# A two-layer attention trunk: the value products of a head pair issued later, its eviction put first on VectorE

## The chip, the cores and the metric

The kernel runs on one core of one Trainium2 chip. The metric is device time in microseconds (us) of one execution; the time before is the median of three runs. The core's engines are TensorE (PE in the profile, with its weight loads as a row of their own, PEld), VectorE (DVE), ScalarE (ACT), GpSimd (POOL) and SyncE (SP), which issues the DMAs.

## The reference, cut to what matters

Two layers run over 512 positions of width 1024. Each layer has a sparse-attention branch (eight heads of 64, in two groups) and a gated linear-attention branch; the change touches the first. Its output per head is a gated sum of three attentions: over compressed keys, over selected blocks, over a window.

```
out = gt[..., 0:1] * o_c + gt[..., 1:2] * o_s + gt[..., 2:3] * o_w
o_nsa = o_nsa * silu(p_nz)
y = m_nsa * (o_nsa @ w_up_nsa) + m_gla * (o_gla @ w_up_gla)
x = x + rms(y @ w_out, g_post)
```

At this length every block is selected and the window covers all earlier positions, so both `o_s` and `o_w` are causal attentions over all 512 positions, with different keys and values.

## The kernel before, in words

All matrices are 32-bit; a product is made with three matmuls, from a high part and a low part (what rounding left over) of each operand: high by high, high by low, low by high (`split3`, lines 175 to 179). A high part is a ScalarE copy, a low part a subtraction on VectorE or GpSimd.

**Attention.** The eight heads are taken in four pairs p (heads p and p + 4). A pair has five steps: `cmp_steps` (compressed keys) and four `attn_steps`, for the two halves ip of the query blocks (i = 0, 1 and i = 2, 3) and the two branches br. `cmp_steps` has three parts: scores and softmax; transposes; and the start of the pair's accumulator `acc` with two matmuls (lines 918, 919). `attn_steps` has three parts: the scores of its first block, those of its second, and the value products (line 998). After the scores `weigh` makes the softmax on VectorE and ScalarE, `turn` transposes it on VectorE into a tile T, writes T to DRAM (line 940) and reads it back rearranged as `W`, a tile of the pool PT, with four DMAs (lines 942, 943). The value products of half 0 are 8 matmuls per branch, those of half 1 are 16; all add into `acc`, a PSUM tile of a pool with one buffer. When the last are done (half 1, branch 1), `acc` is evicted: VectorE multiplies it into `f_` (line 1003), ScalarE takes the high part H (line 1005), GpSimd the low part Lo (line 1006). Pool PT holds two buffers for each half.

**Order.** TensorE's order is the program's, written by hand. The loop at lines 1038 to 1062 goes through 20 steps, n = 5p + m, and calls the parts with `go`; between them `fill` issues matmuls of other projections as gap filler, by a credit in us from the table `FILL`, one row per m, four gaps a row. The other engines' queues (SyncE's too) are ordered by the compiler, which takes what it finds ready in order of priority; priority is program order unless something is put ahead with `tc.high_priority()`. Weight loads (line 136) have three landing buffers, `raw`; one is free when ScalarE and VectorE have split the weights in it (lines 153, 154). They are issued on SyncE, as are the DMAs of `turn`.

**After the loop** the rest of the filler is issued (`need("ug7")`), then the gate projections of the first two output units `un0` and `un1`, then the last pair's second-half values, then the rest of the units. `up` (lines 731 to 746) makes a unit: 24 matmuls of a gate, then 12 of the up-projection over the four pairs' outputs `oTn`, the last pair's (k = 3) last.

Of the kernel before, what the change touches and what calls it, by code (L numbers as in the profile page):

```python
# [9 lines left out]
F32 = mybir.dt.float32  # L10
# [4 lines left out]
OP = mybir.AluOpType  # L15
# [52 lines left out]
def trunk(ctx, tc, x, wpk, sp, gvec, cs, wa, out):  # L68
# [23 lines left out]
    def new(pl, shape=(128, 512), dt=F32, tag=None, bufs=None):  # L92
        cnt[0] += 1
        kw = {} if bufs is None else {"bufs": bufs}
        return sb[pl].tile(list(shape), dt, tag=tag or pl, name=f"{tag or pl}_{cnt[0]}", **kw)

    def ps(tag):
        cnt[0] += 1
        return psp[tag].tile([128, 512], F32, tag=tag, name=f"ps_{tag}_{cnt[0]}")
# [4 lines left out]
    mm, tp = nc.tensor.matmul, nc.tensor.transpose  # L104
    V, A, G = nc.vector, nc.scalar, nc.gpsimd
# [65 lines left out]
    def get(l, n, ahead=2):  # L171
        issue(POS[l, n] + ahead)
        return ready.pop((l, n))

    def split3(o, w, h, first, last):

        mm(o, w[0], h[0], start=first, stop=False)  # L177
        mm(o, w[0], h[1], start=False, stop=False)  # L178
        mm(o, w[1], h[0], start=False, stop=last)  # L179

    def fm(l, n, hT, then):

        w = get(l, n)
        o = ps("mm")
        for k in range(KT):
            if type(w) is list:
                wk = [t[:, k % 4 * 128:(k % 4 + 1) * 128] for t in w[k // 4]]
            else:
                wk = [t[:, k * 128:(k + 1) * 128] for t in w]
            split3(o, wk, hT(k), k == 0, k == KT - 1)  # L190
            if k == KT - 1:
                then(o)
            yield 0.64
# [118 lines left out]
    for l in range(L):  # L312
# [21 lines left out]
        def fill(us):  # L334
            credit[0] += us
            while credit[0] > 0.3 and queue:
                credit[0] -= step(*queue[0])

        def step(name, gen):
            try:  # L340
                return next(gen)
            except StopIteration:
                queue.pop(0)
                done.add(name)
                return 0.0

        def need(name):
            while name not in done:
                step(*queue[0])
# [343 lines left out]
        PR = [[None, None, None, None] for _ in range(4)]  # L693
# [37 lines left out]
        def up(f, gate, wn, src, then):  # L731
            th = []

            def sig(o):
                th.append(new("th"))
                A.activation(th[0], o, AF.Tanh, scale=0.5)

            yield from fm(l, f"{gate}{f}", hT, sig)
            w = get(l, f"{wn}{f}")
            u = ps("mm")  # L740
            for k in range(4):
                sl = slice(k * 128, (k + 1) * 128)
                split3(u, (w[0][:, sl], w[1][:, sl]), src[k], k == 0, k == 3)
                if k == 3:
                    then(th[0], u)
                yield 0.64
# [31 lines left out]
        for f in range(8):  # L778
            put(f"ug{f}", up(f, "mgg", "ug", oTg, take_ug))
# [144 lines left out]
        def turn(p, br, i, pps):  # L924

            ip, n = i // 2, i + 1
            r = (4 * ip + 3) * 64
            if i % 2 == 0:  # L930
                TT[p, br] = new("T", (128, 4, r), tag=f"T{ip}")
            T = TT[p, br]
            t = T[:, :, (i % 2) * i * 64:((i % 2) * i + n) * 64].rearrange("p b (j g q) -> p b j g q", j=n, g=2)
            for g in range(2):
                V.transpose(t[:, :, :, g], pps[g][:, :n * 128].rearrange("p (j b q) -> p b j q", j=n, b=4))  # L935
            if i % 2:
                cnt[0] += 1
                dr = dram.tile([128, 4, r], F32, tag=f"tp{ip}", name=f"tp_{cnt[0]}", bufs=2)
                with tc.issue_after(back[-1]) if back else nullcontext():
                    dma(dr, T)  # L940
                W = PT[p, br, ip] = new("PT", (128, 4, r), tag=f"PT{ip}")
                for b in range(4):
                    back.append(dma(W[b * 32:(b + 1) * 32], dr[:, b].rearrange("(a k) r -> k a r", a=4)).ins)

        def scores(p, i, brs):

            w = (i + 1) * 128
            ww = w * len(brs)  # L950
            both = len(brs) > 1
            nsc[0] += 1
            o = [ps("ts"[nsc[0] % 2]) for _ in range(2)]
            for g in range(2):
                for n in range(2):
                    kn = first[g][:, n].rearrange("p b n -> p (b n)") if both else keys[brs[0]][g][n][:, :w]
                    mm(o[g][:, :ww], PR[p][1][g][:, i * 128:(i + 1) * 128], kn, start=(n == 0), stop=(n == 1))  # L957
            pps = [weigh(p, g, i, brs, o[g]) for g in range(2)]
            turn(p, brs[0], i, [t[0] for t in pps])
            if both:  # L960
                held[p] = [t[1] for t in pps]
# [18 lines left out]
        def attn_steps(p, ip, br):  # L980
            for i in (2 * ip, 2 * ip + 1):
                if i or not br:
                    scores(p, i, (br,) if i else (0, 1))
                else:
                    turn(p, br, i, held.pop(p))
                yield

            acc, W = PR[p][3], PT[p, br, ip]
            i0 = 2 * ip
            for j in range(i0 + 2):  # L990
                for g in range(2):
                    c0 = br * 128 + g * 64
                    if j <= i0:
                        m = W[:, :, :2 * (i0 + 1) * 64].rearrange("p a (i j g q) -> p i a j g q", i=2, g=2, q=32)
                        m, w = m[:, :, :, j, g], 256
                    else:
                        m, w = W[:, :, (2 * j) * 64 + g * 32:(2 * j) * 64 + g * 32 + 32], 128
                    mm(acc[g * 64:(g + 1) * 64, (i0 + 2) * 128 - w:(i0 + 2) * 128],  # L998
                       vsw[j // 2][:, j % 2, c0:c0 + 64], m,
                       start=False, stop=(br == 1 and j == i0 + 1), skip_group_check=True)  # L1000
            if ip == 1 and br == 1:
                f_ = new("p")
                V.scalar_tensor_tensor(f_, acc, 0.5, PR[p][2], op0=OP.mult, op1=OP.mult)
                H, Lo = new("oT", dt=F32R), new("oT", dt=F32R)
                A.copy(H, f_)  # L1005
                G.tensor_tensor(Lo, f_, H.bitcast(F32), op=OP.subtract)  # L1006
                oTn[p] = (H, Lo)
            yield

        steps = []  # L1010
        for p in range(4):
            steps.append((p, cmp_steps, ()))
            steps += [(p, attn_steps, (ip, br)) for ip in range(2) for br in range(2)]
        live = [f(p, *a) for p, f, a in steps]

        def go(n):
            if 0 <= n < len(steps):
                next(live[n])
# [19 lines left out]
        for n in range(len(steps)):  # L1038
            m = n % 5
            f4 = FILL[m]  # L1040
            if m == 0:
                need(f"q{steps[n][0]}")
            if m == 4:
                need(f"nz{steps[n][0]}")
            go(n)
            if m == 3:
                go(n - 5)
                go(n - 4)
            fill(f4[0])
            if m == 2:  # L1050
                go(n - 2)
            fill(f4[1])
            if m != 0:
                go(n)
                fill(f4[2])
            if m == 3:
                go(n - 3)
            if m == 4:
                go(n - 3)
                go(n - 2)  # L1060
            fill(f4[3])
        need("ug7")

        uns = [up(f, "mgn", "un", oTn, take_un(f)) for f in range(8)]
        for f in range(2):
            for k in range(KT):
# [8 lines left out]
        src = x if l == 0 else x1  # L1075
# [6 lines left out]
        for s in range(ST):  # L1082
# [22 lines left out]
            for h, c0, c1 in pieces:  # L1105
                V.scalar_tensor_tensor(xh[h][:, c0:c1], tt[h][:, c0:c1], rs[:, 0:1], xh[h][:, c0:c1],  # L1106
                                       op0=OP.mult, op1=OP.add)
# [80 lines left out]
```

## Time and profile before

| | |
|---|---|
| runs before | 809.73, 810.62, 812.09 us; median 810.62 |
| profiled execution, its own time | 808.68 us |
| its span, first to last instruction | 807.0 us |
| mean granted TensorE clock | 0.997 |
| TensorE busy | 789.5 us (98%) |
| VectorE busy | 553.5 us (69%) |
| ScalarE, GpSimd busy | 354.4 us (44%), 97.6 us (12%) |

Times of single instructions are from the profiled execution, in us from the start of its span. A matmul's busy time overlaps that of the next one, so a run of matmuls is read by the distance of their starts. The two layers show the same pattern; attention is about 142 to 310 in the first and 537 to 704 in the second.

### The profile page before, as it was taken

What the parts mean: (1) busy time and instruction counts of PE and PEld (TensorE: products, weight loads), DVE (VectorE), ACT (ScalarE), POOL (GpSimd) and SP (SyncE); (2) the same over time, 40 slices, a digit from 0 to 9 for tenths busy, and PEclk for the clock granted to TensorE, in tenths of its full rate; (3) what the DMA queues carried; (4) which work ended last, traced back from release to release, by engine and by line L of the source; (5) the groups of instructions that cost most, each with busy time, mean ns of one, the idle gap of its engine ahead of it and who ended that gap; (6) DMA issues with size and microseconds to landing.
All of it is one profiled execution on the core that took longest, in us unless ns stands there. A gap on an engine that the chain in (4) does not pass through costs nothing. (4 is left out here: it accounts for less than half of the span.)

```text
span 807.0 us, 12043 instructions
## 1 busy us (share of the span) xinstructions
PE 789.5 (98%) x4262; PEld 644.4 (80%) x4262; DVE 553.5 (69%) x1274; ACT 354.4 (44%) x731; POOL 97.6 (12%) x117
## 2 busy tenths in 40 slices
PE   8999999999989999999999999999999999999996
PEld 5888788887878887888898878888877788788885
DVE  6753749999998945645574366589999987366223
ACT  5671236554554524442356413556555444245211
POOL 3000024000010102211010102311000101032100
PEclk9999999999999999999999999999999999999998
DMA  6641124367676773446246121234767677545222
GB/s 233 229 147 58 53 67 130 105 191 217 183 236 204 235 227 119 153 153 223 79 129 212 52 78 54 83 114 149 223 201 215 214 212 222 171 157 158 78 105 79
DMA packets 54272, 124.04 MB, mean 154 GB/s; under 512 B 6562, under 2 KB 23490, under 8 KB 54212
## 3 DMA queue, kind: packets, MB, share of 16 engines
q1 hardware_dynamic: 54064, 123.01, 48.4%
q8 instruction: 34, 0.56, 0.3%
q10 hardware_dynamic: 148, 0.27, 0.1%
q14 instruction: 26, 0.21, 0.1%
HBM read 94.94 MB, written 25.17 MB: 149 GB/s over the span
## 5 line engine op out<-in xcount | busy, mean ns | idle before, releaser
L177 PE MATMUL ps_mm<-hT,hl 128*128 128x512 f32 x544 | 217.5, 400 | 0.0
L178 PE MATMUL ps_mm<-hT,hl 128*128 128x512 f32 x544 | 212.5, 391 | 0.0
L179 PE MATMUL ps_mm<-hT,hl 128*128 128x512 f32 x544 | 212.3, 390 | 0.0
L153 ACT CAST hl<-raw 128x1024 fp32r<-128x1024 f32 (+3 forms) x107 | 97.6, 915 | 138.3 <-PE ps_mm L178 99.9
L154 DVE TENSOR_TENSOR hl<-raw,hl 128x1024 fp32r<-128x1024 f32 (+3 forms) x107 | 117.4, 1098 | 47.6 <-ACT hl L153 42.5
L177 PEld LDWEIGHTS ps_mm<-hT,hl 128*128 128x128 f32 x544 | 102.2, 188 | 23.3 <-issue 3.1
L179 PEld LDWEIGHTS ps_mm<-hT,hl 128*128 128x128 f32 x544 | 102.2, 188 | 22.1
L178 PEld LDWEIGHTS ps_mm<-hT,hl 128*128 128x128 f32 x544 | 102.4, 188 | 19.0
L972 ACT ACTIVATE g<-g,sx 128x128 f32<-128x128 f32 (+3 forms) x128 | 71.0, 555 | 67.9 <-DVE sx L970 67.5
L935 DVE STREAM_TRANSPOSE T<-g 128x256 f32<-128x256 f32 (+3 forms) x128 | 58.6, 491 | 0.7
L975 DVE TENSOR_SCALAR g<-g,sx,gt 128x128 f32<-128x128 f32 (+3 forms) x128 | 57.0, 459 | 1.5
L178 PE MATMUL ps_mm<-oT,hl 128*128 128x512 f32 x128 | 50.3, 393 | 1.7 <-POOL oT L1006 1.7
L177 PE MATMUL ps_mm<-oT,hl 128*128 128x512 f32 x128 | 50.9, 398 | 0.0
L179 PE MATMUL ps_mm<-oT,hl 128*128 128x512 f32 x128 | 49.9, 390 | 0.0
L1006 POOL TENSOR_TENSOR oT<-p,oT 128x512 fp32r<-128x512 f32 x8 | 14.3, 1784 | 239.0 <-ACT oT L1005 239.0
L998 PE MATMUL ps_o<-PT,a 128*64 128x256 f32 (+1 forms) x384 | 38.6, 348 | 3.9 <-DMA PT<-tp 3.9
L998 PEld LDWEIGHTS ps_o<-PT,a 128*64 128x64 f32 x384 | 25.4, 137 | 18.3 <-issue 9.4
L200 POOL TENSOR_TENSOR rs<-ms,mhalf 128x1 f32<-128x1 f32 (+1 forms) x24 | 17.2, 719 | 177.0 <-DVE ms L198 175.3
L1026 POOL TENSOR_TENSOR p<-p,g 128x512 f32<-128x512 f32 x16 | 28.0, 1750 | 84.3 <-DVE p L1025 72.7
L970 DVE CUSTOM_DVE_ANT_0 g<-ps_t,cmask 128x256 f32<-128x256 f32 (+3 forms) x64 | 28.8, 477 | 2.3 <-PE ps_t L957 2.2
L970 DVE CUSTOM_DVE_ANT_0 g<-ps_s,cmask 128x128 f32<-128x128 f32 (+3 forms) x64 | 29.0, 481 | 1.7 <-PE ps_s L957 1.7
L178 PEld LDWEIGHTS ps_mm<-oT,hl 128*128 128x128 f32 x128 | 24.1, 188 | 6.5 <-POOL oT L1006 2.3
(269 smaller groups left out, 1313.3 us busy)
## 6 DMA issues: line engine op xcount, KB each, us to landing
raw<-wpk SPq DMA_DIRECT2D x96, 512.0 KB, 3.8
tp<-T SPq DMA_DIRECT2D x16, 896.0 KB, 4.1
PT<-tp SPq DMA_DIRECT2D x64, 224.0 KB, 4.9
raw<-wpk SPq DMA_DIRECT2D x32, 256.0 KB, 3.0
tp<-T SPq DMA_DIRECT2D x16, 384.0 KB, 2.5
PT<-tp SPq DMA_DIRECT2D x64, 96.0 KB, 2.4
a<-wpk SPq DMA_DIRECT2D x16, 256.0 KB, 5.7
p<-x SPq DMA_DIRECT2D x16, 256.0 KB, 2.9
```

Of the source, the lines that this page charges most:

```text
L153: A.copy(H[:, :w], r[:, :w])
L154: V.tensor_tensor(Lo[:, :w], r[:, :w], H[:, :w].bitcast(F32), op=OP.subtract)
L177: mm(o, w[0], h[0], start=first, stop=False)
L178: mm(o, w[0], h[1], start=False, stop=False)
L179: mm(o, w[1], h[0], start=False, stop=last)
L200: G.tensor_tensor(r[:, :n], ms[:, :n], mhalf[:, :n], op=OP.pow)
L935: V.transpose(t[:, :, :, g], pps[g][:, :n * 128].rearrange("p (j b q) -> p b j q", j=n, b=4))
L970: V.tensor_tensor_reduce(pp[:, :w], ob, cmask[:, 512 - w:512], 1.0, -3 * NEG, OP.add, OP.min, sx[:, 0:1])
L972: A.activation(pp[:, :w], pp[:, :w], AF.Exp, bias=sx[:, 0:1], scale=-1.0, accum_out=sx[:, 1:2])
L975: V.tensor_scalar(pp[:, :w], pp[:, :w], sx[:, 2:3], gt[:, i, h * 3 + 1 + br:h * 3 + 2 + br], op0=OP.mult, op1=OP.mult)
L998: mm(acc[g * 64:(g + 1) * 64, (i0 + 2) * 128 - w:(i0 + 2) * 128], vsw[j // 2][:, j % 2, c0:c0 + 64], m, start=False, stop=(br == 1 and j = ...
L1026: G.tensor_tensor(t_, t_, y2[f], op=OP.add)
```

## The change

Four edits. In `up`, the up-projection's three matmuls go in another order: the one with the low part of the pair's output comes last. In `attn_steps`, the eviction on VectorE is put ahead of other work, and the low part of the last pair (p = 3) is made by VectorE in place of GpSimd. In the loop, the first-half values of a pair go from the gap before the last fill of its own m = 4 to the next pair's m = 0, behind the first fill; the second-half values go, in the next pair's m = 3, from before the first two fills to behind them; and the start of `acc` for the new pair goes behind the last fill of m = 3. The last pair's first-half values come right after the loop.

```diff
@@ up @@
-                split3(u, (w[0][:, sl], w[1][:, sl]), src[k], k == 0, k == 3)
+                mm(u, w[0][:, sl], src[k][0], start=(k == 0), stop=False)
+                mm(u, w[1][:, sl], src[k][0], start=False, stop=False)
+                mm(u, w[0][:, sl], src[k][1], start=False, stop=(k == 3))
@@ attn_steps @@
-                V.scalar_tensor_tensor(f_, acc, 0.5, PR[p][2], op0=OP.mult, op1=OP.mult)
+                with tc.high_priority():
+                    V.scalar_tensor_tensor(f_, acc, 0.5, PR[p][2], op0=OP.mult, op1=OP.mult)
                 H, Lo = new("oT", dt=F32R), new("oT", dt=F32R)
                 A.copy(H, f_)
-                G.tensor_tensor(Lo, f_, H.bitcast(F32), op=OP.subtract)
+                (G if p < 3 else V).tensor_tensor(Lo, f_, H.bitcast(F32), op=OP.subtract)
@@ the loop over n, m = n % 5 @@
             go(n)
+            fill(f4[0])
+            if m == 0:
+                go(n - 4)
+                go(n - 3)
+            if m == 2:
+                go(n - 2)
+            fill(f4[1])
             if m == 3:
                 go(n - 5)
                 go(n - 4)
-            fill(f4[0])
-            if m == 2:
-                go(n - 2)
-            fill(f4[1])
             if m != 0:
                 go(n)
                 fill(f4[2])
+            fill(f4[3])
             if m == 3:
                 go(n - 3)
-            if m == 4:
-                go(n - 3)
-                go(n - 2)
-            fill(f4[3])
+        go(len(steps) - 4)
+        go(len(steps) - 3)
         need("ug7")
```

## Rows read from the trace of the kernel before

**Rows 1.** The page, part 1: busy us (share of the span) and instructions.
```profile
PE 789.5 (98%) x4262; PEld 644.4 (80%) x4262; DVE 553.5 (69%) x1274; ACT 354.4 (44%) x731; POOL 97.6 (12%) x117
```

**Rows 2.** Waits of PE: who waited for whom; us in total, times, longest.
```profile
PE ps_o L998 <- DMA PT<-tp: 3.9, 2, 2.1
...
PE ps_mm L178 <- POOL oT L1006: 1.7, 2, 0.8
```

**Rows 3.** Timeline of PE, first layer, third pair's m = 3: start, us, what [idle].
```profile
228.50 1.73 PE L998 MATMUL ps_o<-PT,a 128*64 128x256 f32 x16
232.29 1.74 PE L998 MATMUL ps_o<-PT,a 128*64 128x256 f32 x16 [2.06 <-DMA PT<-tp]
233.96 0.50 PE L177 MATMUL ps_mm<-oT,hl 128*128 128x512 f32 x1
```

**Rows 4.** Timeline of PE, first layer, second pair's m = 3 and on.
```profile
192.09 3.25 PE L998 MATMUL ps_o<-PT,a 128*64 128x256 f32 x32
195.27 0.50 PE L177 MATMUL ps_mm<-hT,hl 128*128 128x512 f32 x1
...
198.15 1.07 PE L957 MATMUL ps_t<-a,a 128*128 128x512 f32 x4
...
201.09 0.41 PE L918 MATMUL ps_o<-p,vbd 128*128 128x512 f32 x1
...
203.64 0.87 PE L957 MATMUL ps_s<-a,a 128*128 128x384 f32 x4
```

**Rows 5.** Timeline of PE, second layer, third pair's m = 3.
```profile
622.90 1.74 PE L998 MATMUL ps_o<-PT,a 128*64 128x256 f32 x16
626.51 1.74 PE L998 MATMUL ps_o<-PT,a 128*64 128x256 f32 x16 [1.87 <-DMA PT<-tp]
```

**Rows 6.** Timeline of SP (its DMA issues), first layer, before that wait.
```profile
218.18 0.34 SPq L940 DMA_DIRECT2D tp<-T  x1
219.09 6.20 SPq L136 DMA_DIRECT2D raw<-wpk  x2
225.40 1.80 SPq L943 DMA_DIRECT2D PT<-tp  x4
```

**Rows 7.** Windows, first layer: length, busy us (instructions) by engine, clock, DMA.
```profile
200.00:250.00 50.00, 47.94 (x262) 38.10 (x260) 47.02 (x135) 25.95 (x63) 3.71 (x2) 1.00 0.65 205
```

**Rows 8.** Timeline of PE, end of the last pair, first layer.
```profile
303.11 3.25 PE L998 MATMUL ps_o<-PT,a 128*64 128x256 f32 x32
306.29 0.50 PE L177 MATMUL ps_mm<-oT,hl 128*128 128x512 f32 x1
...
308.52 0.50 PE L177 MATMUL ps_mm<-oT,hl 128*128 128x512 f32 x1
309.87 0.50 PE L178 MATMUL ps_mm<-oT,hl 128*128 128x512 f32 x1 [0.84 <-POOL oT L1006]
```

**Rows 9.** Timelines of DVE, ACT and POOL, end of the last pair, first layer.
```profile
305.93 1.29 DVE L148 TENSOR_TENSOR a<-raw,a 128x512 fp32r<-128x512 f32 x2
307.13 0.69 DVE L1003 SCALAR_TENSOR_TENSOR p<-ps_o,oT 128x512 f32<-128x512 f32 x1
...
310.71 0.69 DVE L1025 SCALAR_TENSOR_TENSOR p<-th,ps_mm 128x512 f32<-128x512 f32 x1 [2.90 <-PE ps_mm L179]
...
307.85 0.62 ACT L1005 CAST oT<-p 128x512 fp32r<-128x512 f32 x1 [2.06 <-DVE p L1003]
...
308.54 1.27 POOL L1006 TENSOR_TENSOR oT<-p,oT 128x512 fp32r<-128x512 f32 x1 [33.40 <-ACT oT L1005]
```

**Rows 10.** Groups of DVE by line: xcount | busy us, mean ns | idle before.
```profile
L726 DVE TENSOR_TENSOR oT<-p,oT 128x512 fp32r<-128x512 f32 x8 | 5.5, 683 | 0.0
```

**Rows 11.** Timeline of DVE, first layer, around the evictions of the first two pairs.
```profile
200.23 0.66 DVE L1003 SCALAR_TENSOR_TENSOR p<-ps_o,oT 128x512 f32<-128x512 f32 x1
...
202.68 0.68 DVE L970 CUSTOM_DVE_ANT_0 g<-ps_t,cmask 128x512 f32<-128x512 f32 x1
...
235.44 0.65 DVE L1003 SCALAR_TENSOR_TENSOR p<-ps_o,oT 128x512 f32<-128x512 f32 x1
```

## The prediction, as it stood before the changed kernel was run

> **What bounds the kernel now.** The page's first part comes first: TensorE is busy for 789.5 of a span of 807.0 us, 98%, and VectorE, the next, 69% [rows 1]. So TensorE sets the time, and what the change can win is what TensorE now waits for. The profiled execution took 808.68 us, 1.94 below the median of the runs, 810.62. The sum is made against 808.68, and the median is then moved by the same amount.
>
> The second view is TensorE's list of waits. Two of its rows lie where the change is: 3.9 us in two waits for the read-back of transposed weights (DMA PT<-tp, before line 998), and 1.7 us in two waits for GpSimd's low part (line 1006) [rows 2]. The timeline shows that each is one wait in each layer. In the third pair's m = 3 the second pair's second-half values start; after 16 of 32 matmuls TensorE stands for 2.06 us in the first layer [rows 3] and for 1.87 in the second [rows 5]. At the end of the last pair, TensorE idles for 0.84 us before the 11th matmul of the first output unit's up-projection [rows 8].
>
> Why that read-back is late is seen on SyncE: the transposed tile was on its way to DRAM at 218.18, but two weight loads ahead in the queue took from 219.09 to 225.29 to be issued, and only then went the read-back, at 225.40 [rows 6]; what TensorE lacked was there at 232.29 [rows 3]. Weight loads wait for a landing buffer, which VectorE frees, and VectorE is busy for 47.02 of the 50 us from 200 to 250 [rows 7]. So here the arrival hangs on VectorE's queue and not on TensorE, and values that TensorE asks for later will meet an arrival that stays where it is.
>
> **Second-half values, two gaps later.** The instructions are the same; TensorE's order alone changes, and the values issue no DMA and pass no entry of SyncE's or GpSimd's queue. Undisturbed, 32 value matmuls take 3.18 us from their first to the next matmul (192.09 to 195.27) [rows 4]. With the wait it was 228.50 to 233.96, 5.46 [rows 3], so the wait with its restart cost 2.28. In the second layer the restart came after 3.61 (622.90 to 626.51) where it was 3.79 in the first [rows 3, 5], so 2.10. Now the filler of two gaps goes first: in the pair before it took 195.27 to 198.15, 2.88 us [rows 4]. The second 16 will be wanted at 228.50 + 2.88 + 1.59 (half of 3.18) = 232.97, 0.7 us after 232.29; in the second layer at 627.37 against 626.51, 0.9 later. Both waits go, with little to spare: **-2.28 and -2.10**. From below: the arrival moves by as much as the demand and nothing is won. Above, 4.38 is all there is. I take all, since VectorE's work ahead of that load is the same and TensorE's order before it only changes places.
>
> **First-half values, one gap and a step later.** TensorE's list has no wait for them beyond the two above [rows 2]. Later demand can't make one, and their 1.5 us of matmuls is filled around as before: 0. What the later read could hold up is the next pair's read-back into the same buffers, two a half: but the values are now in the first gap of the next pair, ahead of any of its attention scores in TensorE's order, and so of all that its transposes need: 0.
>
> **The eviction and the start of the next accumulator.** There is one such PSUM buffer, so lines 918 and 919 wait for the eviction. Before, the values ended at 195.27 and line 918 came at 201.09, 5.8 us later [rows 4]. VectorE got to the eviction at 200.23, 5.0 us after the values, and was done at 200.89 [rows 11]: 0.2 us to spare. Now values end at 192.09 + 2.88 + 3.18 = 198.15, and line 918 moves behind the last fill, to 203.64 less its own two matmuls, 0.48 (0.24 each, 12 fillers in 2.88 us): 203.16 [rows 4]. If VectorE takes the eviction at the same place in its queue, it is done 2.3 us early; if it falls behind the next scores' two reductions, which start at 202.68, it ends about 204.65 and TensorE waits 1.5 us [rows 11]. It is put first, so 0, with 1.5 in each layer as the upper end. In the second pair it came 1.5 us after the values (235.44 against 233.96) [rows 3, 11], which leaves more room.
>
> **The last pair's tail.** Its values end at 306.29 [rows 8], but VectorE has splits of weights until about 307.13; then come eviction, high part (ended 308.47) and GpSimd's 1.27 us, to 309.81 [rows 9]. The 10th of the unit's 12 matmuls starts at 308.52, the next at 309.87: 1.35, where 0.24 is the pace, so 1.11 are lost [rows 8]; the same in the second layer, where the wait is of one size (1.7 in two, 0.8 the longest) [rows 2]. VectorE makes a low part of this shape in 0.68 [rows 10]. From 308.54 it is done at 309.22. In the new order the low part is wanted one matmul later, at 308.52 + 0.48 = 309.00. That leaves a wait of about 0.25 and wins 0.86. If the eviction goes between the two splits that end at 307.13 (1.29 for both), all 1.11 is won. I take 0.95: **-0.95 twice**. On VectorE the 0.68 is hidden: it then idles for 2.90 us until 310.71 [rows 9]. GpSimd loses work before which it stood 33.40 us idle [rows 9]. The other order of the three matmuls wants the weights' low part 0.24 us earlier; no wait in the list is for it there [rows 2], so 0, and the number of matmuls and weight loads is the same.
>
> **Sum.** -2.28 - 2.10 - 1.90 = -6.28: 808.68 becomes 802.4, and the median 810.62 becomes 804.3. TensorE has no other wait between there and the end, so a layer's gain is kept.
>
> **Rivals.** *A: the wait moves to the start of the accumulator.* For it: 0.2 us to spare before, and a VectorE that is full there [rows 7, 11]. Against it: eviction now goes first. In the fullest pair of each layer it would cost up to 1.5, 3.0 in all: 804.3 to 807.3, still faster.
>
> *B: the read-back is late again.* Spare are only 0.7 and 0.9 us, and the compiler orders SyncE's queue anew; another weight load ahead of it, like the 6.20 us one [rows 6], would keep the wait. Then only the tail is won: 810.62 - 1.90 = 808.7, inside what can't be told apart. Against it: TensorE's demand is the only thing moved. In parts, 805 to 808.7.
>
> *C: VectorE stands at the eviction.* Put first, it can come to the head of VectorE's queue before the values are done, and everything behind it stands s us: softmax, splits, and so SyncE's loads. VectorE is saturated there, so s moves the arrival at 232.29, of which 0.7 us is cover. Before, VectorE showed no idle time ahead of an eviction: it came 5.0 and 1.5 us after the values [rows 3, 4, 11], so the queue was behind by that much, and putting it first uses up just this. If it takes the place that VectorE had reached at 195.27, when the values were done before, s is 198.15 - 195.27 = 2.9, and TensorE waits 2.2: the gain of that wait is gone, 808.7. Each layer loses s - 0.7 against a gain of 3.15, so from s = 3.9 on it is slower than before, and from 5.1 by over 2.4 us: 813. That takes an eviction placed even ahead of where it could have run in the old order. The Trainium skill (PSUM — Partial Sum Buffer, section Engine vs sequencer instructions) calls VectorE's queue strictly first in, first out, which speaks against this edit: by that rule alone nothing could pass a waiting eviction, and the time would be that of this rival for whatever s is. The trace agrees as far as it goes: the ready eviction took its turn, 5.0 us late, behind other work [rows 4, 11].
>
> **How the numbers follow.** A measurement of this kernel can tell about 0.3%, 2.4 us, from no change. Forecast, both waits gone and the tail shortened, 0.65: around 804.3, all of it faster; 803.9 if the tail wins all, and the runs before spread by about a microsecond each way, so 802.8 to 805.5 by itself. A 0.12: faster but for 0.02. B 0.13: 0.06 faster, 0.07 the same. C 0.10: 0.04 the same, 0.06 slower, since its larger sizes are open above. Faster 0.81, same 0.13, slower 0.06. The range runs from 802.8 to 808.0: it takes in the forecast, A, and the partial cases of B and C.
>
> **What the profile will show.** Right: no wait before line 998 but a run of 32 in 3.2 us, no wait before the two accumulator matmuls, VectorE never idle before the eviction, the low part's row on VectorE at 0.68 for two of eight, and a last unit of which the wait is below 0.3. TensorE's busy time stays about 789, and the span shrinks by what it waited. Wrong: a DMA wait still at line 998 (B; SyncE then shows a weight load ahead of the read-back), idle time before lines 918 and 919 (A), or idle time on VectorE released by the value products (C). What would make it wrong altogether is a compiler that orders VectorE or SyncE so differently that weights come late to the filler, for which no wait stands in the list now.

## The result, and the profile after

| | before | after |
|---|---|---|
| median, us | 810.45 (4 runs, one more than ahead of the prediction) | 802.50 (4 runs: 801.41 to 803.11) |
| ratio after / before | | 0.990 [0.9882, 0.9917] |
| profiled execution, us | 808.68 | 803.11 |
| its span, mean granted TensorE clock | 807.0, 0.997 | 801.4, 0.999 |

The kernel is faster by 7.95 us, where 6.3 were forecast. The median lies 0.3 us under the low end of the range. Line numbers move by up to three: values are L1000, the eviction L1006, the accumulator's start L920 and L921, the up-projection L743 to L745.

The page of the kernel after, part 1. TensorE does the same work in a shorter span [rows 1]:

```profile
PE 789.5 (99%) x4262; PEld 644.0 (80%) x4262; DVE 553.3 (69%) x1276; ACT 353.4 (44%) x731; POOL 91.4 (11%) x115
```

TensorE's waits in the kernel after (total, times, longest). The two kinds of [rows 2], read-back and GpSimd's low part, are gone, and the top of the list is now work outside the change:

```profile
PE ps_o L399 <- DVE p L393: 2.6, 1, 2.6
PE ps_t L840 <- DVE p L828: 0.9, 2, 0.5
PE ps_s L801 <- DVE p L828: 0.6, 2, 0.3
```

TensorE's timeline, kernel after, the second pair's second-half values (answers to [rows 3]; last line: the second layer):

```profile
231.57 3.25 PE L1000 MATMUL ps_o<-PT,a 128*64 128x256 f32 x32
234.75 1.20 PE L959 MATMUL ps_s<-a,a 128*128 128x512 f32 x4
...
239.19 0.39 PE L920 MATMUL ps_o<-p,vbd 128*128 128x512 f32 x1
...
623.01 3.25 PE L1000 MATMUL ps_o<-PT,a 128*64 128x256 f32 x32
```

One run of 32 in 3.18 us (231.57 to 234.75) stands where [rows 3] has two runs of 16 with a hole of 2.06.

SyncE's issues, kernel after, the read-back that these values need (answers to [rows 6]):

```profile
219.69 0.34 SPq L942 DMA_DIRECT2D tp<-T  x1
220.27 3.08 SPq L136 DMA_DIRECT2D raw<-wpk  x2
224.56 1.77 SPq L945 DMA_DIRECT2D PT<-tp  x4
```

Two weight loads still stand ahead of it, but they take 3.08 us to be issued where it was 6.20; for the last 1.2 us before 224.56 SyncE waits for the tile's own write to DRAM. Issued at 224.56, the read-back is there at about 231.45 (an estimate) if it takes the 6.89 us of before (225.40 to 232.29) [rows 3, 6]. The second 16 are wanted at 231.57 + 1.59 = 233.16. That leaves 1.7 us, where the prediction had 0.7.

VectorE's timeline, kernel after, three evictions (answers to [rows 11]; the third is one pair later):

```profile
201.21 0.65 DVE L1006 SCALAR_TENSOR_TENSOR p<-ps_o,oT 128x512 f32<-128x512 f32 x1
...
236.08 0.65 DVE L1006 SCALAR_TENSOR_TENSOR p<-ps_o,oT 128x512 f32<-128x512 f32 x1
...
271.24 0.69 DVE L1006 SCALAR_TENSOR_TENSOR p<-ps_o,oT 128x512 f32<-128x512 f32 x1 [0.27 <-PE ps_o L1000]
```

The eviction at 236.08 ends 2.46 us before line 920 wants the buffer at 239.19: no wait there, rival A is absent. At 271.24 VectorE stood for 0.27 us at the head of its queue until the values were done: rival C, but far under the 3.9 us from which the prediction had it slower than before. The Trainium skill (PSUM — Partial Sum Buffer, section Engine vs sequencer instructions) calls that queue strictly first in, first out; the 0.27 us fits it.

TensorE's timeline, kernel after, the last pair's tail (answers to [rows 8]):

```profile
301.19 3.25 PE L1000 MATMUL ps_o<-PT,a 128*64 128x256 f32 x32
304.37 0.50 PE L743 MATMUL ps_mm<-oT,hl 128*128 128x512 f32 x1
...
306.93 0.40 PE L744 MATMUL ps_mm<-oT,hl 128*128 128x512 f32 x1
307.32 0.50 PE L745 MATMUL ps_mm<-oT,hl 128*128 128x512 f32 x1
307.66 0.39 PE L743 MATMUL ps_mm<-oT,hl 128*128 128x512 f32 x1
```

VectorE there (answers to [rows 9]):

```profile
305.20 0.69 DVE L1006 SCALAR_TENSOR_TENSOR p<-ps_o,oT 128x512 f32<-128x512 f32 x1
306.58 0.69 DVE L1009 TENSOR_TENSOR oT<-p,oT 128x512 fp32r<-128x512 f32 x1 [0.69 <-ACT oT L1008]
```

The 12 matmuls of the unit take 3.29 us (304.37 to 307.66), where they took 4.16 (306.29 to 310.45): 0.87 won, 0.85 in the second layer (4.15 to 3.30).

**Where the time went, between the two profiled executions.** The same instructions on TensorE in both give the stretches: the first layer's attention starts 0.32 us later (142.46, 142.78), ahead of all that was changed; in four profiles of the kernel before the same instruction comes between 141.01 and 142.73, so this is scatter. By the last pair's values it is 1.92 earlier (303.11, 301.19): -2.24 in the loop. By the second layer's first scores it is 2.63 earlier (542.65, 540.02): -0.71 over the tail and what follows, where a wait for VectorE (line 223) grew from 0.42 to 0.61 us. By the last pair's values there, 4.69 (697.32, 692.63): -2.06. By the end, 5.57: -0.88. The sum of the prediction, -6.28, was made for this pair. The other 2.4 us of the 7.95 are between profiled execution and median: before, the profiled execution was 1.77 under its median; after, 0.61 over it. 5.57 + 1.77 + 0.61 = 7.95.

### The profile page after: what moved, and what is told of

The parts are those of the page before. It is cut to its first block, busy times and chain, and to the rows that moved or that the text cites. A ratio compares the mean times of both kernels' runs of the same rounds, so it can differ in the third digit from the quotient of the medians.

```text
span 801.4 us, 12035 instructions
## 1 busy us (share of the span) xinstructions
PE 789.5 (99%) x4262; PEld 644.0 (80%) x4262; DVE 553.3 (69%) x1276; ACT 353.4 (44%) x731; POOL 91.4 (11%) x115
## 5 line engine op out<-in xcount | busy, mean ns | idle before, releaser
L743 PE MATMUL ps_mm<-oT,hl 128*128 128x512 f32 x128 | 50.5, 394 | 0.0
L745 PE MATMUL ps_mm<-oT,hl 128*128 128x512 f32 x128 | 50.0, 391 | 0.0
L1000 PE MATMUL ps_o<-PT,a 128*64 128x256 f32 (+1 forms) x384 | 38.1, 348 | 0.0
L1000 PEld LDWEIGHTS ps_o<-PT,a 128*64 128x64 f32 x384 | 25.0, 137 | 14.9 <-issue 5.0
L745 PEld LDWEIGHTS ps_mm<-oT,hl 128*128 128x128 f32 x128 | 24.0, 188 | 6.0 <-DVE oT L1009 0.9
L148 DVE TENSOR_TENSOR oT<-raw,oT 128x512 fp32r<-128x512 f32 x32 | 22.2, 721 | 9.4 <-ACT oT L147 9.3
```

The costliest lines, as they stand in the source:

```text
L743: mm(u, w[0][:, sl], src[k][0], start=(k == 0), stop=False)
L745: mm(u, w[0][:, sl], src[k][1], start=False, stop=(k == 3))
```

## The experiments

Two theories of the 7.95 us. The first: it is the idle time in the rows, as in the prediction's sum, and the rest is chance. The rival: a wait also costs TensorE's clock behind it, so that waits removed pay more than their length. And one question on the parts: is the loop's gain that of the second-half values alone? Differences below are medians against the runs of the kernel before on the same chip.

**1. The kernel before again.** No edit.

> The kernel before, unchanged, profiled once more. Changed and unchanged kernel differ by 7.95 us in the medians (810.45 to 802.5), but by 5.57 in the two profiled executions (808.68 to 803.11). Theory 1, the profiled execution of before was a quick one: the waits for the read-back before line 998 are longer in other executions, so this one takes 810 to 812 us and its two waits sum to 5 to 7 us where they were 3.9. Theory 2, the waits at line 998 are the same in each execution (3.9 us within 0.5) and the runs differ elsewhere, as in the first stage's loads or in the time around the span.

Measured: 810.34 against 811.21, ratio 0.9986 [0.9963, 1.0009]; the kernel's 8 times go from 807.19 to 813.51. Its profiled execution took 811.26. TensorE's timeline shows three waits before line 998, 6.2 us in all, where [rows 2] have two with 3.9:

```profile
232.92 1.73 PE L998 MATMUL ps_o<-PT,a 128*64 128x256 f32 x16 [2.44 <-DMA PT<-tp]
...
270.88 1.74 PE L998 MATMUL ps_o<-PT,a 128*64 128x256 f32 x16 [1.43 <-DMA PT<-tp]
...
629.15 1.73 PE L998 MATMUL ps_o<-PT,a 128*64 128x256 f32 x16 [2.31 <-DMA PT<-tp]
```

This is theory 1: 2.3 us more of waits and 2.6 us more time, with the mean clock at 0.999, so without the clock. The waits of one kernel differ between executions, and one profiled execution is not the median.

**2. The loop's edits alone**; `up`, the priority and the low part as before.

```diff
-            if m == 3:
-                go(n - 5)
-                go(n - 4)
             fill(f4[0])
+            if m == 0:
+                go(n - 4)
+                go(n - 3)
...
             fill(f4[1])
+            if m == 3:
+                go(n - 5)
+                go(n - 4)
...
+            fill(f4[3])
             if m == 3:
                 go(n - 3)
-            if m == 4:
-                go(n - 3)
-                go(n - 2)
-            fill(f4[3])
+        go(len(steps) - 4)
+        go(len(steps) - 3)
```

> The loop's edits alone: values and the start of the accumulator in the new places; the order of the three matmuls, the eviction's priority and GpSimd's low part as before. By the prediction's terms -4.4 us (2.28 + 2.10); by the two profiles, where the same stretches gave 2.24 and 2.05, -4.3. If the medians' surplus of 1.7 us over the predicted 6.3 belongs to the waits for the read-back (theory 1), -6.0. If it belongs to an edit that was put at nothing (eviction first, low part off GpSimd), -4.3 here and the surplus is missing.

803.62 against 811.21, ratio 0.9902 [0.988, 0.9924]: -7.6. No wait at line 998; the wait for GpSimd's low part stays (1.7 in two). The gain is larger than either size expected, and nearly all of it is the loop's.

**3. The tail's edits alone.** Loop and priority as before.

```diff
-                split3(u, (w[0][:, sl], w[1][:, sl]), src[k], k == 0, k == 3)
+                mm(u, w[0][:, sl], src[k][0], start=(k == 0), stop=False)
+                mm(u, w[1][:, sl], src[k][0], start=False, stop=False)
+                mm(u, w[0][:, sl], src[k][1], start=False, stop=(k == 3))
...
-                G.tensor_tensor(Lo, f_, H.bitcast(F32), op=OP.subtract)
+                (G if p < 3 else V).tensor_tensor(Lo, f_, H.bitcast(F32), op=OP.subtract)
```

> The matmul order and the last low part on VectorE alone; the loop and the eviction as before. By the prediction -1.9 us, by the two profiles (0.7 and 0.9 in the stretch from the last pair's values on) -1.6. If the surplus belongs here, -3.3 or more. The two waits of 2 us before line 998 stay.

809.24, ratio 0.9976 [0.996, 0.9992]: -2.0, where 1.90 was forecast. The waits for the read-back are as before (3.6 in two). Loop and tail together, -9.6, are within the noise of the whole (-8.7 on the same chip, experiment 4).

**4. After, without the priority.**

```diff
-                with tc.high_priority():
-                    V.scalar_tensor_tensor(f_, acc, 0.5, PR[p][2], op0=OP.mult, op1=OP.mult)
+                V.scalar_tensor_tensor(f_, acc, 0.5, PR[p][2], op0=OP.mult, op1=OP.mult)
```

> The changed kernel with the eviction at its ordinary priority. By the prediction the priority was to keep the start of the next accumulator free (at most 1.5 us in each layer without it) and won nothing by itself: between the changed kernel's time and 3 us above it, so -5 to -8 against before. In the changed kernel the eviction still came 2.75 us after the values in the second pair, and ended 1.6 us before the accumulator's start, so I expect no difference that can be measured: -7.5 to -8. If priority carried the surplus, -6.

802.52, ratio 0.9885 [0.9862, 0.9908]: -8.7, the interval of the kernel after overlaps it. The eviction keeps its places, and the 0.27 us of VectorE stands there too. The priority is worth nothing here: its 0 in the sum was right.

**5. The wait filled with work.** The kernel before, with 8 matmuls by a tile of zeros between the two branches' values, in the third pair only. The sum in the accumulator is unchanged.

```diff
-        vbd = [const((128, 128), F32R, f"vbd{i}") for i in range(2)]
+        vbd = [const((128, 128), F32R, f"vbd{i}") for i in range(3)]
...
                 go(n - 5)
+                if n == 13:
+                    for _ in range(8):
+                        mm(PR[1][3], vbd[2], hT(0)[0], start=False, stop=False, skip_group_check=True)
                 go(n - 4)
```

> The kernel before with 8 matmuls more in each layer: zeros times an input, added to the second pair's accumulator between the two branches' second-half values, where TensorE waits (8 times 0.23 is 1.8 us of work in a wait of 1.5 to 2.4). Each wait shrinks by what is put into it. Theory 1, the surplus over the predicted 6.3 us comes from TensorE's clock, which falls in many executions of before (its mean granted clock over 31 of them is 0.9960, over 12 of the three kernels without the waits 0.9981, and 0.0021 of 810 us is 1.7 us): with the idle time filled the clock stays up, so the mean clock is 0.998 and the time 1.7 us below before although there is more work, about 809.5. Theory 2, the clock has nothing to do with these waits: time as before within 0.5 us and clock 0.996.

809.17 against 810.50, ratio 0.9985 [0.9971, 0.9999]: -1.3 with more work. TensorE's timeline of this kernel:

```profile
227.61 1.74 PE L998 MATMUL ps_o<-PT,a 128*64 128x256 f32 x16
229.28 2.12 PE L1050 MATMUL ps_o<-hT,vbd 128*128 128x512 f32 x8
231.33 1.73 PE L998 MATMUL ps_o<-PT,a 128*64 128x256 f32 x16
...
235.87 1.07 PE L957 MATMUL ps_s<-a,a 128*128 128x512 f32 x4
```

The zeros take 2.05 us (229.28 to 231.33) where TensorE stood for 2.06 [rows 3], and from the second 16 to the next scores it is 4.54 us, as in the profile of before (232.29 to 236.83). So against that one profile nothing is won; against the median 1.3 is. Its mean clock is 0.9982 over 12 runs; the kernel before has 0.9958 over 79 runs, all that stood beside the experiments. SyncE's queue is the one of before (two weight loads in 6.19 us, then the read-back, at 224.35), so the edit did not bring the data earlier. This speaks for the clock, though the interval ends close to 1.

**6. Second-half values earlier**, before the last fill of m = 2. TensorE asks sooner for what is already late.

```diff
-            if m == 3:
-                go(n - 5)
-                go(n - 4)
             fill(f4[0])
...
                 fill(f4[2])
+            if m == 2:
+                go(n - 4)
+                go(n - 3)
             if m == 3:
                 go(n - 3)
```

> The kernel before with the second-half values one place earlier: before the last fill of m = 2 in place of after the first scores of m = 3, some 2 us sooner for TensorE. Where the arrival hangs on VectorE's and SyncE's queues and stays, the second pair's wait grows from 2 to 4 us in each layer, and the first pair's values, which now have 0.3 us to spare, wait 1.7: +7 to +8 us in all by waits alone. If the clock falls after such idle time (theory 1), there are stretches of this trace with a granted clock near 0.5, a mean clock below 0.995, and the time is 2 us or more above what the waits sum to. If the arrival moves with the demand, no change.

806.28, ratio 0.9946 [0.9928, 0.9964]: -4.2, where +7 to +8 was expected, and not a longer wait. TensorE's timeline of this kernel:

```profile
190.75 1.74 PE L998 MATMUL ps_o<-PT,a 128*64 128x256 f32 x16
193.85 1.74 PE L998 MATMUL ps_o<-PT,a 128*64 128x256 f32 x16 [1.36 <-DMA PT<-tp]
...
227.98 3.25 PE L998 MATMUL ps_o<-PT,a 128*64 128x256 f32 x32
```

The wait of [rows 3] is gone, though the values come earlier; the pair before waits 1.36 instead. On SyncE the read-back went out at 222.50 instead of 225.40 [rows 6], behind weight loads of 2.15 us instead of 6.20. The arrival does not stay where it is when TensorE's order changes.

**7. One gap instead of two.** The kernel after, with the second-half values behind the first fill only.

```diff
+            if m == 3:
+                go(n - 5)
+                go(n - 4)
             fill(f4[1])
-            if m == 3:
-                go(n - 5)
-                go(n - 4)
```

> The changed kernel with the second-half values behind one fill of m = 3 in place of two, so about 1.4 us sooner. In the changed kernel the second 16 matmuls of the third pair's m = 3 start 1.8 and 1.6 us after their data has landed. So 0.2 us to spare on the profiled times, and waits of up to 1 us in executions where the read-back is slower: within 1 us of the changed kernel, -7 to -8.5 against before, with a mean clock of 0.998 since the waits are short. If one gap had been as good as none, -2.

803.27, ratio 0.9913 [0.9886, 0.9939]. A rest of the wait is back, 1.1 us in two (0.31 in the first layer, 0.75 in the second), with a mean clock of 0.9985. The second gap buys the rest and cover; from the medians alone it can't be told from after.

**8. Read-backs issued by GpSimd**, so that no weight load stands ahead of them. The kernel before with one edit.

```diff
-                    back.append(dma(W[b * 32:(b + 1) * 32], dr[:, b].rearrange("(a k) r -> k a r", a=4)).ins)
+                    back.append(nc.gpsimd.dma_start(W[b * 32:(b + 1) * 32], dr[:, b].rearrange("(a k) r -> k a r", a=4)).ins)
```

> The kernel before with the four read-back DMAs of each transposed tile issued by GpSimd in place of SyncE; everything else as before. If the read-back is late because it stands in SyncE's queue behind weight loads that wait for a buffer (6.20 us in the first layer), the two waits before the values go and the kernel gains what the loop's edits gain, 5 to 7 us, less what GpSimd's own issue costs. If the transfer itself is slow, the waits stay at 2 us each and the time is as before.

807.54, ratio 0.9961 [0.9945, 0.9977]: -3.0. The wait of [rows 3] is gone (32 in one run at 230.37). GpSimd's row for this read-back shows that it now waits for the tile's write to DRAM alone:

```profile
224.27 2.23 POOL L943 DMA_DIRECT2D PT<-tp  x4 [9.32 <-DMA tp<-T]
```

It goes out 5.16 us after that write (219.11 to 224.27), where it was 7.22 (218.18 to 225.40) [rows 6]: 2.06 less, as long as the wait was. So SyncE's queue was its cause. But the pair before waits 1.30 us, and another wait is new (L912 for VectorE, 1.2 us): 3.1 us in three stay at line 998.

**9 and 10. The kernel before, two more profiles.** No edit, one execution each.

> The kernel before once more, to see an execution in which TensorE's clock falls; in about half of the 57 executions so far its mean granted clock was 0.995 or less, and no profile kept shows where. Theory 1: the rows show a granted clock near 0.5 for some us right behind a wait for the read-back, and the mean clock's shortfall against 0.998 is what this time lies above 808 or so. Theory 2: the clock falls elsewhere (at the start, or at the seam of the layers), with no wait of the values near it.

> As the run before it: a second look, since an execution with a mean clock of 0.998 or 0.999 would show nothing.

810.46 and 810.29. Windows of the first (length, busy us of PE, PEld, DVE, ACT, POOL, then the granted clock, DMA share, GB/s):

```profile
225.00:230.00 5.00, 3.77 (x27) 2.59 (x25) 4.86 (x18) 2.58 (x7) 0.00 (x0) 1.00 1.00 274
230.00:235.00 5.00, 4.24 (x21) 3.13 (x22) 4.43 (x14) 1.97 (x5) 0.00 (x0) 0.67 0.62 220
235.00:240.00 5.00, 5.00 (x23) 4.16 (x22) 3.75 (x10) 2.43 (x6) 1.80 (x1) 0.99 0.60 187
...
625.00:630.00 5.00, 3.36 (x19) 2.44 (x20) 4.57 (x16) 1.31 (x4) 0.00 (x0) 0.76 0.78 259
630.00:635.00 5.00, 5.00 (x22) 4.10 (x21) 3.73 (x7) 2.38 (x4) 1.81 (x1) 0.90 0.46 157
```

TensorE's timeline of the same execution:

```profile
227.04 1.73 PE L998 MATMUL ps_o<-PT,a 128*64 128x256 f32 x16
230.76 2.39 PE L998 MATMUL ps_o<-PT,a 128*64 128x256 f32 x16 [1.99 <-DMA PT<-tp]
...
233.67 0.63 PE L178 MATMUL ps_mm<-oT,hl 128*128 128x512 f32 x1
234.10 0.63 PE L179 MATMUL ps_mm<-oT,hl 128*128 128x512 f32 x1
...
236.87 1.07 PE L957 MATMUL ps_s<-a,a 128*128 128x512 f32 x4
```

Behind a wait of 1.99 us the clock falls from its upper level, 2.4 GHz, to the lower, 1.2: by half microseconds the granted clock is 1.00 up to 231.5 and 0.50 from 232.0 to 235.0. The matmuls go at 0.43 us each (233.67 to 234.10) instead of 0.23. From the second 16 to the next scores it is 6.11 us (230.76 to 236.87), where it was 4.54 without a fall: the wait cost 1.57 more. In the second layer it is 6.09 (626.64 to 632.73), 1.55 more. In the other execution one of the two waits brought it, in the second layer:

```profile
626.34 3.24 PE L998 MATMUL ps_o<-PT,a 128*64 128x256 f32 x16 [2.81 <-DMA PT<-tp]
...
632.36 1.07 PE L957 MATMUL ps_s<-a,a 128*128 128x512 f32 x4
```

6.02 us, 1.48 more; the first layer's wait of 1.97 left the clock at 1.00. The profile of before that the prediction used had two such waits and no fall: its clock over the fullest 50 us is 1.00 [rows 7], and what its mean of 0.997 lacks lies behind 800 us, where TensorE has nearly no work left.

**11. The first-half values alone**, the move whose worth the prediction put at 0.

```diff
             fill(f4[0])
+            if m == 0:
+                go(n - 4)
+                go(n - 3)
...
-            if m == 4:
-                go(n - 3)
-                go(n - 2)
             fill(f4[3])
+        go(len(steps) - 4)
+        go(len(steps) - 3)
```

> The kernel before with the first-half values alone moved to the next pair's first gap. The prediction put this at 0. By theory 1 the two waits of the second-half values stay, with the clock at 0.996 and the time as before within 0.7 us. If this move carried part of the gain, through another order of VectorE's or SyncE's queue, it is 1 us or more faster and the waits of the second-half values are shorter or gone.

806.37 against 810.15, ratio 0.9945 [0.9928, 0.9962]: -3.8. TensorE's timeline of this kernel, the second pair's second-half values:

```profile
227.82 1.73 PE L998 MATMUL ps_o<-PT,a 128*64 128x256 f32 x16
230.55 1.74 PE L998 MATMUL ps_o<-PT,a 128*64 128x256 f32 x16 [1.00 <-DMA PT<-tp]
```

They stand where they stood, and the wait is 1.00 instead of 2.06 (1.6 in the second layer). SyncE's order is the same, 6.20 us of weight loads and then the read-back, but at 223.90 instead of 225.40. VectorE is ahead: it does the eviction of [rows 11] 7.0 us after its values began (191.48 to 198.49), where it was 8.1 (192.09 to 200.23). Five of six runs have a mean clock of 0.999.

**12. The second-half values and the accumulator's start alone**, the edit to which the prediction gave all of the loop's gain.

```diff
-            if m == 3:
-                go(n - 5)
-                go(n - 4)
             fill(f4[0])
             if m == 2:
                 go(n - 2)
             fill(f4[1])
+            if m == 3:
+                go(n - 5)
+                go(n - 4)
...
-            if m == 3:
-                go(n - 3)
...
             fill(f4[3])
+            if m == 3:
+                go(n - 3)
```

> The kernel before with the second-half values and the accumulator's start in their new places, the first-half values, the tail and the eviction as before. The prediction gave this edit the whole gain of the loop, 4.4 us. By what the runs have shown since (all of the loop's edits -7.6 us, the first-half values alone -3.8), if TensorE's demand alone matters, the demand is 2.9 us later, the waits of 2 to 2.8 us go and the clock stays at 0.998: -6 to -7.5, and the first-half move adds at most 1.5. If VectorE's order, which the first-half move changed, is what brings the data in time, waits of 0.5 us or more remain before the values and it is -4 or less.

818.14 against 810.76, ratio 1.0105 [1.0083, 1.0126]: slower by 7.4. TensorE's waits and, below, its timeline in this kernel:

```profile
PE ps_o L998 <- DMA PT<-tp: 7.6, 5, 3.4
```

```profile
207.35 0.87 PE L998 MATMUL ps_o<-PT,a 128*64 128x256 f32 x8
211.17 1.55 PE L998 MATMUL ps_o<-PT,a 128*64 128x256 f32 x8 [2.95 <-DMA PT<-tp]
212.65 0.80 PE L177 MATMUL ps_mm<-hT,hl 128*128 128x512 f32 x1
...
234.54 3.25 PE L998 MATMUL ps_o<-PT,a 128*64 128x256 f32 x32
```

The second-half values run as one, as forecast (234.54). But now the *first*-half values, at the end of m = 4, stand for 2.95 us, and the clock falls behind them (0.66 from 210 to 215 us). SyncE's issues in this kernel:

```profile
200.53 0.34 SPq L940 DMA_DIRECT2D tp<-T  x1
200.91 5.33 SPq L136 DMA_DIRECT2D raw<-wpk  x2
206.35 1.79 SPq L943 DMA_DIRECT2D PT<-tp  x4
```

In the kernel before, the same read-back:

```profile
200.34 0.34 SPq L940 DMA_DIRECT2D tp<-T  x1
202.05 0.35 SPq L136 DMA_DIRECT2D raw<-wpk  x1
202.69 1.74 SPq L943 DMA_DIRECT2D PT<-tp  x4
```

One more weight load is ahead of it, and it goes out 3.7 us later. The kernel after has this order as well (SyncE, first two lines); there the first-half values run only at 212.89 (TensorE, last line):

```profile
201.69 5.33 SPq L136 DMA_DIRECT2D raw<-wpk  x2
207.13 1.79 SPq L945 DMA_DIRECT2D PT<-tp  x4
...
212.89 1.52 PE L1000 MATMUL ps_o<-PT,a 128*64 128x256 f32 x16
```

Sixteen in one run, without a wait. The two moves pay together: +7.4 and -3.8 alone, -7.6 both. The accumulator's start went with the second-half move; which of the two turns the queue was not tried.

## Why the prediction missed, and where it was right

**The step that failed: "The sum is made against 808.68, and the median is then moved by the same amount."** That keeps the 1.94 us between profiled execution and median constant. It isn't constant, since the change takes away what makes it, and two terms are missing from the sum.

The first is waits that are longer in other executions. The four profiles of the kernel before have 3.9, 6.2, 4.0 and 4.8 us of them, 4.7 in the mean, 0.8 more than the profile of the sum. The second is TensorE's clock. In the profiled execution the waits cost their length alone; in others the clock falls behind a wait, and each of the three falls measured cost 1.5 to 1.6 us more. Of 79 executions of the kernel before, the 17 with a mean clock of 0.998 or more average 809.31 us (the 31 with 0.997 or more, 809.33); all together average 810.66. So some 0.6 of the 1.94 us is there at full clock too, and some 1.35 goes with the clock. Two more readings of the clock's part are near that: filling the wait with useless work gave -1.3, and the kernels without long waits (after, the loop's edits alone, without the priority) have a mean clock of 0.998, the kernel before 0.9958, and 0.0023 of 810 is 1.9 us. That last reading is rough, since the mean clock counts the kernel's end too, as in the profile of before.

From the full-clock executions the same sum would give 809.3 - 6.3 = 803.0, within the range and 0.5 from the measured 802.5. The Trainium skill (TensorE: Matmul & The Clock Gate, section HAM oscillation — how this bites in real kernels) describes waits for DMA between groups of matmuls after which the clock is down, in its case at every one of them. The windows at 0.67 and 0.76 right behind the 1.99 us waits agree with the fall; the waits of 2.06 and 1.87 in the profile of before and of 2.44 and 2.31 in experiment 1 show that here it doesn't follow each one. Shown are falls behind the waits, that filling one raises the clock and lowers the time, and that the waits differ between executions. The split of the surplus (7.95 over 6.28) between the two terms is an estimate, and 0.6 us of it is only that after's profiled execution lay above its median.

**The second step that failed, inside a right total: "I take all, since VectorE's work ahead of that load is the same and TensorE's order before it only changes places", with 0 for the first-half values.** Apart, the first-half values are worth -3.8 and the second-half values +7.4. Both sizes are near what waits and clock give: for the first half waits of 2.6 instead of 3.9 us and a mean clock of 0.9987, some -1.3 - 2.3; for the second half 7.6 instead of 3.9 and 0.9908, some +3.7 + 4.0 (estimates from one profile and the runs' clocks). The compiler orders VectorE's and SyncE's queues anew for each order of TensorE, so there is no "arrival that stays where it is". What was called rival B, a weight load put ahead of a read-back, did come, but ahead of the first half's, and the move that was put at nothing is what covers it. That the loop's total came out as forecast between the profiles was luck: without the move called worthless, the edit that was to bring it makes the kernel slower. "Later demand can't make one" held; that later demand can take away a wait which another edit makes was not looked for.

**The sizes.** For the loop -2.28 and -2.10 were forecast, -2.24 and -2.06 measured between the profiles. For the tail -0.95 twice (0.86 to 1.11): 0.87 and 0.85 in the unit, the low end; VectorE's order did not put the eviction ahead of the two splits that end at about 305.2. "TensorE has no other wait between there and the end" was a misreading: three waits for VectorE of 0.3 to 0.4 us each stand between the layers' attention, and of the first layer's 0.87 only 0.71 arrived. Eviction and accumulator 0: right, with and without the priority. Rival A has no trace; rival C's 0.27 us stands without the priority too. GpSimd's low part left the list of waits.

**Open.** Why a wait of about 2 us brings a fall in one execution (1.99, twice) and none in another (1.97, 2.06, 2.44); why the waits differ between executions of one kernel; and why the compiler's order comes out so differently for moves of one or two gaps. No kernel tried beats the one after: without the priority (802.52) it is the same.

## What to carry to other kernels

Before a sum is moved from a profile to the median, see from further profiles whether its waits are as long as in other executions, and whether the clock falls behind them there: a wait that goes takes both along. A read-back that stands behind waiting weight loads in one queue is late by what those wait for, and a change of TensorE's order reorders that queue, so an edit is judged with the queue that comes out, and its parts may not add. Moving consumers later all along, in step, is what gave cover for both halves here.

## What the runs showed of the hardware that was not expected

TensorE's clock fell to its lower level behind single waits of 1.99 us (twice) and 2.81 us, in the middle of a kernel that is 98% busy: 5-us windows at 0.67, 0.76 and 0.66, and 1.48 to 1.57 us lost for each; waits of 1.87 to 2.44 us in other executions brought no fall. In the first of them the matmuls were back at their pace 4.5 us after the wait's end (230.76 to 235.26). Eight matmuls by zeros in that hole raised the mean clock from 0.9958 to 0.9982 and made the kernel 1.3 us faster (ratio 0.9985 [0.9971, 0.9999]). A weight load that waited on SyncE held the read-back behind it by 2.06 us. GpSimd's low part took 1.30 us each in the kernel after (six), and up to 2.16 us in the kernel before.
